# A two-layer diffusion backbone on one core: token tiles transposed in pairs, the second layer's gate made ahead of its attention, modulation columns by transposes

## The chip, the core and the metric

The kernel runs on one core of a Trainium2 chip. A core has five engines that run their own queues of instructions in order: TensorE (PE in the profile, with its weight loads shown apart as PEld), VectorE (DVE), ScalarE (ACT), GpSimd (POOL) and SyncE (SP), which here only issues DMA transfers. They work on SBUF, the on-chip memory of 128 partitions, and on PSUM, the banks that matmuls write. An engine that waits for another waits on a semaphore, and everything queued behind the waiting instruction on its engine waits with it.

The metric is the device time of one execution in microseconds, here 831.68 us as the median of three runs.

## The reference

The input is 512 latent tokens `x` and 256 context tokens `ctx`, 1024 wide, and two conditioning vectors, one for the latents and one for the context. There are two layers. Both modulate a normalised token, mix tokens by attention, gate the result, project it and add it back:

```python
h  = rms_norm(x,  pre_g[i]) * (1.0 + scale)  + shift     # shift, scale, gate = silu(c) @ ada_w[i] + ada_b[i]
hc = rms_norm(xc, pre_g[i]) * (1.0 + cscale) + cshift
...
x = x + gate * rms_norm(y, post_g[i])
if not last:
    xc = xc + cgate * rms_norm(yc, post_g[i])
```

The first layer's mixer is differential attention: 8 heads, each with two softmaxes of width 64, whose outputs are subtracted. The second is grouped-query attention with 8 query heads and 2 key/value heads of width 128, with a norm and a rotary position on queries and keys. In both a SiLU gate path `z` of the branch width multiplies the heads' output ahead of the output projection. In the second layer only the latents are wanted, the context gives keys and values alone. All inputs and the output are float32.

The modulation (`silu(c) @ ada_w[i] + ada_b[i]`) has three thirds: shift and scale, which the kernel needs as columns (features on partitions), and the gate, which it needs as a row that is the same on all partitions.

## The kernel before

**Arithmetic.** A float32 product is made of three float32r products: each operand is split into a high part (a cast to float32r) and a low part (the difference), and high by high, high by low and low by high are summed in PSUM. The helper `mm3` issues the three, and they are the rows L148, L149 and L150 of the profile. A weight comes in as float32 (`raw`, L209, a pool of two buffers named `raw` in SBUF), is cast on ACT (`whi`, L211), and its low part is made on POOL or DVE (`wlo`, L205). The stream of weights has a fixed order; a weight is loaded as soon as one of its slots is released.

**Order of the work.** Most of the code is generators that yield after each piece. In each layer a planner (`flow`) merges streams of steps: scores of a head (S), transposes of probabilities (T), products with V (M), odd steps (X), and one for the gate or modulation (A in the first layer, Y in the second). Each step has due times and lags against other steps; the time in between is filled with pieces of projections. The order of instructions on each engine is then set by the compiler's scheduler from that code and its priorities. It is fixed before the kernel runs.

**PSUM.** Four banks `bk` (68 to 71 in the listings below) are handed out in turn by `trp()` (for one use) and `pj()` (held until `close`). Two double banks `sc` (72 and 73) are handed out in turn by `sc2()`, and carry the attention scores.

**Modulation of both layers.** A section of the modulation is computed with `silu(c)` in one of four bands of 32 columns, so that its result stands in eight rows out of 128 (two vectors in each of four bands). `ada_red` (first layer, at the start; L498) and `ada1_finish` (second layer, inside the first layer's attention; L715) turn this into columns: a matmul of each 128x128 block against `sel32`, a 128x2 selector in float32, sums the bands. The profile counts each of those 16 and 16 float32 matmuls twice (x32 and x32). `gate0_finish` (L980) makes the first layer's gate as a row on all partitions by a float32 matmul against a 128x128 selector `selb`, two halves by two vectors, again counted twice (x8).

**Between the layers.** The output projection of layer one runs in three column windows (256, 256 and 512 wide). In the last, for each token tile m of 128 tokens (0 to 3 latents, 4 and 5 context), `resid_a` and `resid_b` norm the projection, add it to the token and norm that (`u`, L1169; `xn`, L1189, in two buffers). `h1_tr(m, j)` then transposes half of the tile, four blocks of 128x128, to one bank `bk` (L1196), modulates them with two instructions on DVE (L1202) and two on ACT (L1204), casts the result (L1206, ACT) and takes the low part (L1207, DVE): 12 calls. Those for tiles 0 to 3 stand in the loop over the last window, two tiles late; those for tiles 4 and 5 stand in the table `KV` as `('t', 4)` and `('t', 5)`, between the key (`'k'`) and value (`'v'`) projections of the six tiles and the transposes of keys (`'c'`).

**Second layer.** After the keys and values the weights' memory of that stage is released and a new SBUF pool, `t1q`, is opened in its place. The first pair of query heads is projected (`q_proj(0)`: matmuls to a `bk` bank, norm on ACT, rotary products `ta` and `tb` on DVE, L1241 and L1243, after which the bank is closed). Then `flow` runs the attention: `s1_units` makes scores to an `sc` tile, takes the row maximum on DVE (L1383), multiplies it (L1386), applies the exponential on ACT (`p`, L1389) and normalises. The gate of layer two is made on DVE: `gate1_part` loads 512 KB of `ada_w` (L1434) to one of the two `raw` buffers and multiplies its two 128x512 blocks by a column of `silu(c)` into an accumulator (L1442, L1444); four such parts make a half. `gate1_finish` sums a half over partitions by two matmuls, and adds and multiplies two rows (L1454, L1456). These ten steps are the stream Y, due behind the score steps 1, 3, 5, ... 19 of 32. The gate is first read by the output projection of layer two.

## Time and profile before

| what | value |
|---|---|
| median of three runs | 831.68 us (831.57 to 832.28) |
| profiled execution | 830.24 us |
| its span | 828.4 us (1.84 us of the execution lie outside) |
| PE busy | 794.2 us, 96% |
| DVE, ACT, POOL busy | 483.8, 456.6 and 435.5 us |
| granted PE clock over the span | 0.99 of full |
| layer one ends, last output window and first residuals begin | about 500 us |
| keys and values of layer two | 539 to 581 us |
| first queries | 581 to 605 us |
| attention of layer two | 605 to 780 us |

In the profile's rows `out<-in` names the tiles with their numbers left out, so that `h` is the high or low part of a token block, `hf` its float32 form, `gate` the accumulator of a gate, `sm` any small column. An arrow behind the idle time (`<-ACT p L1389`) names what ended the wait. Matmuls overlap, so the spacing of two starts says more of a matmul's price than its duration.

### The profile page before, as it was taken

The numbers are of one execution on the slowest core, as the hardware profiler recorded it, in microseconds if no ns is written. First come the engines' busy times: TensorE is split into PE (matmuls) and PEld (weight loads), VectorE is DVE, ScalarE is ACT, GpSimd is POOL, SyncE is SP. The second block draws the span as 40 slices with busy tenths as digits, with TensorE's granted clock in tenths as the row PEclk, the third lists the DMA queues.
The fourth block names the chain that finished last, engine by engine and source line by source line (L and its number), as shares of the span: only waits on it lengthen the run. The fifth ranks groups of instructions, "written<-read, shape, count | busy, mean of one in ns | idle before, by whom it ended". The sixth has DMA issues, their size and how long they took to land. (4 is left out here: it accounts for less than half of the span.)

```text
span 828.4 us, 14363 instructions
## 1 busy us (share of the span) xinstructions
PE 794.2 (96%) x5436; PEld 700.7 (85%) x5436; DVE 483.8 (58%) x909; ACT 456.6 (55%) x997; POOL 435.5 (53%) x612
## 2 busy tenths in 40 slices
PE   7999999999999999999999999889998989999997
PEld 4788897898878898878988898789998879899986
DVE  3745567664767426765278743764266676665634
ACT  5524457564665625855467643754464656666631
POOL 1124847965576752867633203575876746734201
PEclk9999999999999999999999999999999999999999
DMA  9924301212143331414210051121232340301112
GB/s 344 355 72 140 102 14 64 80 63 78 64 122 109 115 99 42 166 57 154 96 51 27 27 204 51 51 85 51 82 101 75 95 155 6 103 26 30 65 34 101
DMA packets 35236, 77.76 MB, mean 94 GB/s; under 512 B 3424, under 2 KB 10336, under 8 KB 35168
## 3 DMA queue, kind: packets, MB, share of 16 engines
q1 hardware_dynamic: 31600, 71.71, 26.0%
q10 hardware_dynamic: 3568, 5.16, 1.8%
q8 instruction: 42, 0.69, 0.4%
q14 instruction: 26, 0.21, 0.1%
HBM read 70.56 MB, written 2.10 MB: 88 GB/s over the span
## 5 line engine op out<-in xcount | busy, mean ns | idle before, releaser
L205 POOL TENSOR_TENSOR wlo<-raw,whi 128x256 fp32r<-128x256 f32 x196 | 148.4, 788 | 117.9 <-ACT whi L211 82.0
L148 PE MATMUL bk<-whi,h 128*128 128x256 f32 (+1 forms) x592 | 177.1, 301 | 5.6 <-DVE u L1169 2.0
L149 PE MATMUL bk<-wlo,h 128*128 128x256 f32 (+1 forms) x592 | 175.9, 298 | 0.3 <-DVE wlo L205 0.3
L150 PE MATMUL bk<-whi,h 128*128 128x256 f32 (+1 forms) x592 | 174.4, 298 | 0.8 <-DVE h L1207 0.8
L148 PE MATMUL bk<-h,whi 128*128 128x512 f32 (+2 forms) x416 | 147.1, 354 | 2.9 <-ACT sq L943 1.5
L149 PE MATMUL bk<-h,whi 128*128 128x512 f32 (+2 forms) x416 | 145.0, 349 | 0.0
L150 PE MATMUL bk<-h,wlo 128*128 128x512 f32 (+2 forms) x416 | 144.8, 349 | 0.0
L148 PEld LDWEIGHTS bk<-whi,h 128*128 128x128 f32 x592 | 112.3, 190 | 15.6 <-issue 3.6
L149 PEld LDWEIGHTS bk<-wlo,h 128*128 128x128 f32 x592 | 112.4, 190 | 4.0 <-DVE wlo L205 0.5
L150 PEld LDWEIGHTS bk<-whi,h 128*128 128x128 f32 x592 | 111.6, 189 | 4.8 <-DVE h L1207 1.2
L219 POOL TENSOR_SCALAR p<-p,sm 128x768 f32<-128x768 f32 (+1 forms) x80 | 67.2, 842 | 67.6 <-DVE sm L1390 23.4
L148 PEld LDWEIGHTS bk<-h,whi 128*128 128x128 f32 x416 | 78.4, 188 | 17.1 <-issue 5.4
L211 ACT CAST whi<-raw 128x1024 fp32r<-128x1024 f32 x64 | 67.3, 1051 | 46.2 <-PE bk L149 15.2
L150 PEld LDWEIGHTS bk<-h,wlo 128*128 128x128 f32 x416 | 78.3, 188 | 8.2 <-issue 1.3
L149 PEld LDWEIGHTS bk<-h,whi 128*128 128x128 f32 x416 | 78.5, 189 | 6.5 <-issue 0.3
L854 ACT ACTIVATE p<-sc,sm 128x768 f32<-128x768 f32 (+1 forms) x68 | 59.6, 880 | 29.7 <-DVE sm L851 29.6
L851 DVE TENSOR_REDUCE sm<-sc 128x1 f32<-128x768 f32 (+1 forms) x68 | 60.6, 918 | 17.0 <-PE sc L846 17.0
L205 POOL TENSOR_TENSOR sz<-sz,za 128x192 f32<-128x192 f32 (+1 forms) x48 | 32.1, 689 | 40.8 <-ACT za L185 40.8
L862 DVE SCALAR_TENSOR_TENSOR p<-p,sm,p 128x768 f32<-128x768 f32 (+1 forms) x34 | 39.0, 1146 | 24.3 <-POOL p L219 23.5
L914 ACT CAST ah<-bk 128x512 fp32r<-128x512 f32 x56 | 31.8, 590 | 31.6 <-PE bk L911 27.3
L915 DVE TENSOR_TENSOR al<-bk,ah 128x512 fp32r<-128x512 f32 x56 | 37.5, 684 | 17.5 <-ACT ah L914 17.3
L846 PE MATMUL sc<-qk,qk 64*128 64x384 f32 (+1 forms) x396 | 46.3, 360 | 1.4 <-ACT p L854 1.4
(236 smaller groups left out, 1683.6 us busy)
## 6 DMA issues: line engine op xcount, KB each, us to landing
raw<-in_a_w SPq DMA_DIRECT2D x28, 512.0 KB, 3.5
araw<-in_ada_w SPq DMA_DIRECT2D x12, 1024.0 KB, 5.3
raw<-in_b_w SPq DMA_DIRECT2D x20, 512.0 KB, 3.5
ag<-in_ada SPq DMA_DIRECT2D x16, 512.0 KB, 7.7
raw<-in_w_out SPq DMA_DIRECT2D x16, 512.0 KB, 3.5
sw<-qr ACTq DMA_DIRECT2D x32, 128.0 KB, 2.1
raw<-in_ada_w SPq DMA_DIRECT2D x8, 512.0 KB, 4.0
xnt<-in_xlT SPq DMA_DIRECT2D x4, 512.0 KB, 5.6
```

What stands on the lines that cost most here:

```text
L148: nc.tensor.matmul(o, ahi, bhi, start=start, stop=False)
L149: nc.tensor.matmul(o, ahi, blo, start=False, stop=False)
L150: nc.tensor.matmul(o, alo, bhi, start=False, stop=stop)
L205: eng.tensor_tensor(dst[:, i:i + n], a[:, i:i + n], b[:, i:i + n], op)
L211: nc.scalar.copy(hi, r)
L219: (nc.vector if eng == "v" else nc.gpsimd).tensor_scalar(dst, src, s_, 1.0, ALU.mult, ALU.mult)
L846: prev = nc.tensor.matmul(sc[m][:, j if nk == T else m, :w], a[r, tok], b[r, c], start=i == 0, stop=i == 2)
L851: nc.vector.tensor_reduce(mx, scv, AX.XY if nk == T else AX.X, ALU.max, negate=True)
L854: nc.scalar.activation(pv_, scv, AF.Exp, bias=mx, accum_out=l[:, m:m + 1])
L862: nc.vector.scalar_tensor_tensor(ps_[0], pt, r, ps_[0], ALU.mult, ALU.add)
L914: nc.scalar.copy(ah, tr)
L915: nc.vector.tensor_tensor(al, tr, f32(ah), ALU.subtract)
```

## The change

The diff has four parts.

1. `row_cols` takes the place of the `sel32` matmuls in `ada_red` and `ada1_finish`: it transposes each 128x128 block, and DVE sums the four bands from PSUM into a small tile.
2. `gate0_finish` splits its row into a high and a low float32r part (ACT and DVE, to tiles of the tag `tmp`, of which there are three, shared with other users) and issues two float32r matmuls where one float32 matmul stood. `selb` becomes float32r.
3. `h1_tr(p, j)` works on a pair of token tiles: eight transposes to a double bank `sc`, modulation 256 wide, and cast and low part for two blocks of features at a time. The calls for pairs 0 and 1 stand in the loop at its fourth and sixth tile, those for pair 2 in `KV` as `('t', 0)` and `('t', 1)`, where the second number is now the half. The order of keys and values in `KV` changes with it.
4. The eight calls of `gate1_part` are issued right behind `q_proj(0)`, ahead of the planner, with two buffers `gw` of their own in the pool `t1q`. `gate1_finish` stays in the stream Y, due behind score steps 6 and 12.

```diff
...
-KV = (('k', 0), ('k', 1), ('k', 2), ('k', 3), ('t', 4), ('v', 0), ('v', 1), ('k', 4), ('t', 5), ('c', 0), ('k', 5), ('c', 1), ('c', 2), ('c', 3), ('v', 3), ('v', 2), ('v', 5), ('c', 4), ('v', 4), ('c', 5))
+KV = (('k', 0), ('k', 1), ('k', 2), ('t', 0), ('k', 3), ('t', 1), ('v', 0), ('v', 1), ('c', 0), ('v', 2), ('c', 1), ('k', 4), ('c', 2), ('k', 5), ('c', 3), ('v', 3), ('v', 4), ('c', 4), ('v', 5), ('c', 5))
...
-GOFF = 1
-GSTEP = 2
+GFIN = (6, 12)
...
     nc.vector.tensor_copy(s32[:, :, 0:2], scv)
     sel32 = cp.tile([P, 2], F32, name="sel32", bufs=1)
     nc.vector.tensor_reduce(sel32, ident.rearrange("p (j r) -> p r j", j=4)[:, 0:2, :], AX.X, ALU.add)
-    selb = [cp.tile([P, P], F32, name=f"selb{v}", bufs=1) for v in range(2)]
+    selb = [cp.tile([P, P], F32R, name=f"selb{v}", bufs=1) for v in range(2)]
     for v in range(2):
         nc.vector.tensor_copy(selb[v], sel32[:, v:v + 1].to_broadcast([P, P]))
 
...
         row = st.tile([P, 512], F32, tag="row", name=nm("row"), bufs=1)[:, :n * P]
         nc.scalar.copy(row, o)
         close(o)
-        o = trp()
+        mods_set(k0, nb, row_cols(row, n).rearrange("p (w k v) -> p w v k", w=2, k=nb))
+
+    def row_cols(r, n):
+        o = trp()[:, :n * P]
         for b in range(n):
-            nc.tensor.matmul(o[:, b * 2:b * 2 + 2], row[:, b * P:(b + 1) * P], sel32, start=b == 0, stop=b == n - 1)
-        ov_ = o[:, :2 * n].rearrange("p (w k v) -> p w v k", w=2, k=nb)
-        mods_set(k0, nb, ov_)
+            nc.tensor.transpose(o[:, b * P:(b + 1) * P], r[:, b * P:(b + 1) * P], ident)
+        cols_ = small(2 * n)
+        nc.vector.tensor_reduce(
+            cols_.rearrange("p (b r) -> p b r", b=n), o.rearrange("p (b j r) -> p b r j", j=4, r=32)[:, :, 0:2, :], AX.X, ALU.add)
+        return cols_
 
     def mods_set(k0, nb, src):
         ks = slice(k0, k0 + nb)
...
 
         def ada1_finish(layer, sec):
             r = rows.pop((layer, sec))
-            o = trp()
-            for b in range(4):
-                nc.tensor.matmul(o[:, 2 * b:2 * b + 2], r[:, b * P:(b + 1) * P], sel32, start=b == 0, stop=b == 3)
-            ov_ = o[:, :8].rearrange("p (k v) -> p v k", v=2)
+            ov_ = row_cols(r, 4).rearrange("p (k v) -> p v k", v=2)
             mod_cols(layer, sec % 2, sec // 2, lambda v: ov_[:, v, :])
 
         qk, pend, qk_t = {}, {}, {}
...
             sl = slice(half * 512, half * 512 + 512)
             b = bcast(ada_b[0, 2 * D + half * 512:2 * D + half * 512 + 512])
             g = bcast(post_g[0, sl])
+            rh, rl = (t0.tile([P, 512], F32R, tag="tmp", name=nm("rg"), bufs=3) for _ in range(2))
+            nc.scalar.copy(rh, r)
+            nc.vector.tensor_tensor(rl, r, f32(rh), ALU.subtract)
             for v in range(2):
                 o = trp()
-                nc.tensor.matmul(o, selb[v], r, start=True, stop=True)
+                nc.tensor.matmul(o, selb[v], rh, start=True, stop=False)
+                nc.tensor.matmul(o, selb[v], rl, start=False, stop=True)
                 nc.vector.tensor_tensor(gate0[v][:, sl], o, b, ALU.add)
                 nc.vector.tensor_tensor(gate0[v][:, sl], gate0[v][:, sl], g, ALU.mult)
 
...
         nc.gpsimd.tensor_scalar(t, xd, r, 1.0, ALU.mult, ALU.mult)
         xn[m] = t
 
-    def h1_tr(m, j):
-        v = 0 if m < NQ else 1
-        tr = trp()
-        for k in range(4):
-            nc.tensor.transpose(tr[:, k * P:(k + 1) * P], xn[m][:, (j * 4 + k) * P:(j * 4 + k + 1) * P], ident)
-        hf = bp.tile([P, 4, P], F32, tag="hf", name=nm("hf"), bufs=1)
+    def h1_tr(p, j):
+        v = 0 if 2 * p < NQ else 1
+        tr = sc2().rearrange("p j (k n) -> p (j k) n", n=2 * P)
+        for i in range(2):
+            for k in range(4):
+                nc.tensor.transpose(tr[:, k, i * P:(i + 1) * P], xn[2 * p + i][:, (j * 4 + k) * P:(j * 4 + k + 1) * P], ident)
+        hf = bp.tile([P, 4, 2 * P], F32, tag="hf", name=nm("hf"), bufs=1)
         for k in range(4):
             kt = j * 4 + k
-            src, s_, h_ = tr[:, k * P:(k + 1) * P], mods[:, 1, v, 1, kt:kt + 1], mods[:, 1, v, 0, kt:kt + 1]
+            s_, h_ = mods[:, 1, v, 1, kt:kt + 1], mods[:, 1, v, 0, kt:kt + 1]
             if k < HFD:
-                nc.vector.tensor_scalar(hf[:, k, :], src, s_, h_, ALU.mult, ALU.add)
+                nc.vector.tensor_scalar(hf[:, k, :], tr[:, k, :], s_, h_, ALU.mult, ALU.add)
             else:
-                nc.scalar.activation(hf[:, k, :], src, AF.Identity, scale=s_, bias=h_)
-        hs = h1hi[:, j * 4:j * 4 + 4, m * P:(m + 1) * P]
-        nc.scalar.copy(hs, hf)
-        nc.vector.tensor_tensor(h1lo[:, j * 4:j * 4 + 4, m * P:(m + 1) * P], hf, f32(hs), ALU.subtract)
+                nc.scalar.activation(hf[:, k, :], tr[:, k, :], AF.Identity, scale=s_, bias=h_)
+        for a in (0, 2):
+            sl = slice(2 * p * P, 2 * p * P + 2 * P)
+            hs = h1hi[:, j * 4 + a:j * 4 + a + 2, sl]
+            nc.scalar.copy(hs, hf[:, a:a + 2])
+            nc.vector.tensor_tensor(h1lo[:, j * 4 + a:j * 4 + a + 2, sl], hf[:, a:a + 2], f32(hs), ALU.subtract)
 
     for i, m in enumerate(order):
         o = pj(n)
         run(out_proj(o, ghi, glo, w, m, n, 0, 4))
-        if i >= 2:
-            h1_tr(order[i - 2], 0)
+        if i in (3, 5):
+            h1_tr(i // 2 - 1, 0)
         run(out_proj(o, ghi, glo, w, m, n, 4, 8))
         resid_a(m, o)
-        if i >= 2:
-            h1_tr(order[i - 2], 1)
+        if i in (3, 5):
+            h1_tr(i // 2 - 1, 1)
         resid_b(m)
     ws.release(*wout_keys(0, c, n))
     pool_h.close()
...
         wv = None
         for what, m in KV:
             if what == "t":
-                hot(h1_tr, m, 0)
-                hot(h1_tr, m, 1)
+                hot(h1_tr, 2, m)
             elif what == "c":
                 k_tr(*ktr.pop(0))
             else:
...
 
         def gate1_part(half, k2):
             acc = gate1[:, half * 512:half * 512 + 512]
-            gw = wp.tile([P, 1024], F32, tag="raw", name=nm("raw"), bufs=2)
+            gw = t1q.tile([P, 1024], F32, tag="gw", name=nm("gw"), bufs=2)
             nc.sync.dma_start(
                 gw.rearrange("p (k n) -> p k n", k=2),
                 ada_w[1, k2 * 256:(k2 + 1) * 256, 2 * D + half * 512:2 * D + half * 512 + 512].rearrange("(k p) n -> p k n", p=P),
...
 
         add(q_proj(0))
         drain()
+        for i in range(8):
+            gate1_part(i // 4, i % 4)
         for kind, i in fill1:
             add({"q": q_proj, "z": z1_proj}[kind](i))
         S_, T_, M_, X_ = [], [], [], []
...
                 if h == KT - 1 and ch == 1:
                     T_.append(Step(tail1, 0.0, [(M_[-1], 0.0), (u[-1], 0.0)]))
                 pv1_steps(h, at, ch, u[-1], T_, M_)
-        Y_ = []
-        for i in range(10):
-            f = (lambda i=i: gate1_part(i // 5, i % 5)) if i % 5 < 4 else (lambda i=i: gate1_finish(i // 5))
-            Y_.append(Step(f, 0.9 if i % 5 == 4 else 0.0, [(S_[min(31, GOFF + GSTEP * i)], 0.0)], hot=False))
+        Y_ = [Step(lambda i=i: gate1_finish(i), 0.9, [(S_[GFIN[i]], 0.0)], hot=False) for i in range(2)]
         flow(1, [S_, T_, M_, X_, Y_])
         drain()
         w_o = w_o[0]
```

Three places show what this does to the queues. In the listings, tiles keep their numbers, and lines are each kernel's own (L148 and L1196 of before are L147 and L1202 of after).

PE, before, at the end of the last output window: `bk_71` is the projection of token tile 5, the transposes of `xn_5776` are those of tile 3.

```order
L150 MATMUL bk_71<-whi_5554,h_5072 128x512
L148 MATMUL bk_71<-whi_5554,h_5213 128x512
L149 MATMUL bk_71<-wlo_5555,h_5213 128x512
L150 MATMUL bk_71<-whi_5554,h_5214 128x512
L1196 MATMUL bk_70<-ident,xn_5776 128x128 x4
L148 MATMUL bk_71<-whi_5913,h_671_5297 128x256
L149 MATMUL bk_71<-wlo_5914,h_671_5297 128x256
L150 MATMUL bk_71<-whi_5913,h_672_5298 128x256
L148 MATMUL bk_71<-whi_5913,h_671_5297 128x256
```

PE, after, at the same place: `bk_69` is the projection of tile 5, `xn_5718` and `xn_5796` are tiles 2 and 3, and the matmuls to `bk_71` are the first key projection.

```order
L1202 MATMUL sc_73<-ident,xn_5796 128x128 x4
L149 MATMUL bk_69<-whi_5584,h_5102 128x512
L147 MATMUL bk_69<-whi_5584,h_5243 128x512
L148 MATMUL bk_69<-wlo_5585,h_5243 128x512
L149 MATMUL bk_69<-whi_5584,h_5244 128x512
L1202 MATMUL sc_72<-ident,xn_5718 128x128 x4
L1202 MATMUL sc_72<-ident,xn_5796 128x128 x4
L147 MATMUL bk_71<-whi_5923,h_684_5327 128x256
L147 MATMUL bk_70<-whi_5923,h_684_5327 128x256
```

The transposes of tiles 2 and 3 now go to the double banks `sc`, close together, and the last of them stand ahead of the first key projection as a group of eight.

SP, before, behind the weights of the first query pair: `raw_6820` and `raw_6999` are loads of the gate, the others weights of layer two.

```order
L209 DMA raw_6618<-in_b_w 128x1024
L209 DMA raw_6627<-in_b_w 128x1024
L209 DMA raw_6676<-in_b_w 128x1024
L1434 DMA raw_6820<-in_ada_w 128x2x512
L209 DMA raw_6904<-in_b_w 128x1024
L209 DMA raw_6913<-in_b_w 128x1024
L1434 DMA raw_6999<-in_ada_w 128x2x512
```

SP, after, from the same place on: `gw` are the loads of the gate.

```order
L1441 DMA gw_6636<-in_ada_w 128x2x512
L1441 DMA gw_6640<-in_ada_w 128x2x512
L208 DMA raw_6618<-in_b_w 128x1024
L1441 DMA gw_6644<-in_ada_w 128x2x512
L208 DMA raw_6627<-in_b_w 128x1024
L1441 DMA gw_6648<-in_ada_w 128x2x512
L1441 DMA gw_6652<-in_ada_w 128x2x512
L208 DMA raw_6708<-in_b_w 128x1024
L1441 DMA gw_6656<-in_ada_w 128x2x512
L1441 DMA gw_6660<-in_ada_w 128x2x512
```

The gate's first two loads now stand ahead of three weights behind which the first stood before, and seven of its eight loads come with three weights, where before two came with five.

DVE, before, from the third query tile of the first pair (`ta_6572`) on: the gate's first part (`gate_5296` from `raw_6820`) comes behind the fourth (`ta_6612`).

```order
L1241 TENSOR_TENSOR ta_6572<-bk_71,ropeb 128x256
L1243 TENSOR_TENSOR tb_6573<-bk_71,ropeb 128x2x64 x2
L1325 TENSOR_SCALAR qrs_6567<-qrs_6567 128x2
L1241 TENSOR_TENSOR ta_6612<-bk_69,ropeb 128x256
L1243 TENSOR_TENSOR tb_6613<-bk_69,ropeb 128x2x64 x2
L1325 TENSOR_SCALAR qrs_6607<-qrs_6607 128x2
L1442 TENSOR_SCALAR gate_5296<-raw_6820,scol 128x512
L1444 SCALAR_TENSOR_TENSOR gate_5296<-raw_6820,scol,gate_5296 128x512
L1344 TENSOR_TENSOR ql_6653<-bk_68,qh_6652 128x512
```

DVE, after, from the second query tile of the first pair: the multiplications of the gate, `gate_5326` from `gw`, stand between the rotary products of the query tiles.

```order
L1449 TENSOR_SCALAR gate_5326<-gw_6636,scol 128x512
L1451 SCALAR_TENSOR_TENSOR gate_5326<-gw_6636,scol,gate_5326 128x512
L1249 TENSOR_TENSOR ta_6532<-bk_71,ropeb 128x256
L1251 TENSOR_TENSOR tb_6533<-bk_71,ropeb 128x2x64 x2
L1451 SCALAR_TENSOR_TENSOR gate_5326<-gw_6640,scol,gate_5326 128x512 x2
L1249 TENSOR_TENSOR ta_6572<-bk_69,ropeb 128x256
L1251 TENSOR_TENSOR tb_6573<-bk_69,ropeb 128x2x64 x2
L1332 TENSOR_SCALAR qrs_6527<-qrs_6527 128x2
L1451 SCALAR_TENSOR_TENSOR gate_5326<-gw_6644,scol,gate_5326 128x512
L1332 TENSOR_SCALAR qrs_6567<-qrs_6567 128x2
L1451 SCALAR_TENSOR_TENSOR gate_5326<-gw_6644,scol,gate_5326 128x512
L1451 SCALAR_TENSOR_TENSOR gate_5326<-gw_6648,scol,gate_5326 128x512
```

Three parts of the gate and half of the fourth now stand ahead of the fourth query tile, where before none did; all eight stand ahead of the first maximum of scores, where before one did.

## The prediction

> **What bounds the kernel now.** I read the page's first lines, then a table of windows cut by stage, then what TensorE waited for, then the order of time at the costliest wait.
>
> ```profile
> span 828.4 us, 14363 instructions
> PE 794.2 (96%) x5436; PEld 700.7 (85%) x5436; DVE 483.8 (58%) x909; ACT 456.6 (55%) x997; POOL 435.5 (53%) x612
> ```
>
> TensorE is busy 96% of the span and idle for 34 us. Nothing else is near full. So two things shorten the kernel: less work on TensorE where it is never idle, or an end to its waits. The windows show which stage offers which (columns: window, length, then busy time of each engine, granted clock last but two).
>
> ```profile
> core 0: us, PE busy (x) PEld busy (x) DVE busy (x) ACT busy (x) POOL busy (x), PEclk, DMA share, GB/s
> 16.40:60.00 43.60, 42.59 (x289) 32.78 (x290) 24.62 (x52) 17.98 (x35) 12.60 (x16) 0.96 0.67 243
> 160.00:430.00 270.00, 267.47 (x1892) 230.49 (x1892) 155.24 (x280) 155.28 (x323) 168.44 (x219) 1.00 0.29 96
> 500.00:539.00 39.00, 36.18 (x171) 29.06 (x169) 21.99 (x35) 20.31 (x53) 18.61 (x36) 1.00 0.16 55
> 539.00:581.10 42.10, 39.34 (x317) 37.80 (x317) 22.37 (x57) 22.29 (x63) 26.63 (x39) 1.00 0.21 67
> 581.10:604.80 23.70, 23.70 (x179) 22.60 (x178) 7.19 (x22) 11.25 (x32) 20.73 (x34) 1.00 0.27 90
> 604.80:780.00 175.20, 166.46 (x1132) 155.59 (x1131) 115.94 (x233) 108.52 (x231) 96.62 (x131) 0.99 0.24 73
> ```
>
> Layer one's attention (160 to 430) has TensorE busy 99%: only its own work counts. The last output window and the keys and values (500 to 581) leave 2.8 and 2.8 us idle. The first queries (581 to 604.8) leave none, with DVE at 7.2 of 23.7 us. The second attention leaves 8.7 us. What TensorE waited for there:
>
> ```profile
> PE sc L148 <- ACT p L1389: 6.0, 3, 3.1
> PE bk L148 <- DVE u L1169: 2.0, 2, 1.3
> PE bk L148 <- ACT sz L1363: 1.6, 1, 1.6
> PE bk L148 <- ACT hf L1204: 1.1, 3, 0.6
> PE bk L1196 <- DVE u L1169: 0.9, 1, 0.9
> PE bk L150 <- DVE h L1207: 0.8, 2, 0.4
> PE bk L148 <- ACT h L1206: 0.6, 1, 0.6
> ```
>
> The rows give total, count and longest. Rows two, four, five, six and seven are the stage between the layers: 5.4 us. The other two are the second attention. The largest single wait, in order of time, with two windows behind it:
>
> ```profile
> 620.77 2.15 DVE L1444 SCALAR_TENSOR_TENSOR gate<-raw,scol,gate 128x512 f32<-128x512 f32 x2 [0.74 <-DMA raw<-in_ada_w]
> ...
> 624.58 0.77 DVE L1444 SCALAR_TENSOR_TENSOR gate<-raw,scol,gate 128x512 f32<-128x512 f32 x1
> 625.28 0.74 DVE L1386 TENSOR_TENSOR sm<-sm,qrs 128x1 f32<-128x1 f32 x1
> 625.94 0.76 DVE L1444 SCALAR_TENSOR_TENSOR gate<-raw,scol,gate 128x512 f32<-128x512 f32 x1
> 626.62 0.94 DVE L1383 TENSOR_REDUCE sm<-sc 128x1 f32<-128x768 f32 x1
> 627.19 0.58 PE L148 MATMUL sc<-kh,qh 128*128 128x384 f32 x1 [3.09 <-ACT p L1389]
> 627.20:629.00 1.80, 1.80 (x6) 1.80 (x7) 1.80 (x6) 0.00 (x0) 0.51 (x1) 0.54 0.64 223
> 629.00:631.00 2.00, 2.00 (x12) 2.00 (x11) 1.60 (x9) 0.79 (x1) 1.70 (x3) 0.56 0.15 61
> ```
>
> Here DVE waits 0.74 us for a load of the gate and multiplies for 3.7 us, and the column L1386 for the exponential stands behind it. TensorE waits 3.09 us for a score bank, and then its clock is granted at 0.54 and 0.56 for 3.8 us, which loses another 1.7.
>
> **Part one, modulation columns.**
>
> ```profile
> 308.88 0.40 PE L150 MATMUL bk<-h,wlo 128*128 128x512 f32 x1
> 309.11 0.95 PE L715 MATMUL bk<-sel,arow 128*128 128x2 f32 x8
> 309.92 0.64 PE L911 MATMUL bk<-ident,p 128*128 128x128 f32 x4
> 310.31 0.48 PE L148 MATMUL bk<-h,whi 128*128 128x512 f32 x1
> ```
>
> From start to start, four columns (eight issues) take 0.81 us and four transposes 0.39. Each `ada1_finish` therefore saves 0.42 on TensorE: four of them 1.7 us, all in busy time. The Trainium skill, page "TensorE: Matmul & The Clock Gate", section "Part 4: PE-mode transpose", gives about 275 ns for a 128x128 transpose in a kernel; taken as a price each, an estimate from that figure is 4.4 us for sixteen against 3.2 now, a loss of 1.2 us and a forecast of 822.3 in place of 819.4. The trace lets a run of four last 0.64 us but starts the next work after 0.39, so I go by the trace. The sums that DVE adds (eight, over 32 or fewer numbers per partition) read little; the nearest rows are L1386's 0.74 and L1383's 0.94, so at most 1 us each, and DVE has 115 us free in that window. In layer one nothing waits soon for layer two's columns, so they cost nothing; without that cover they would add at most 4.
>
> At the start, five `ada_red` make 16 columns: 1.7 us of TensorE at the same saving. Their results are waited for, and DVE's sum lengthens that chain, so the bounds are −1.7 and +1; I take −0.6, since TensorE is busy 42.59 of 43.60 us in that window.
>
> **Part two, the first gate.**
>
> ```profile
> 207.71 1.13 PE L980 MATMUL bk<-arow,selb 128*128 128x512 f32 x2
> 208.67 0.60 PE L911 MATMUL bk<-ident,p 128*128 128x128 f32 x4
> ```
>
> A float32 matmul of 512 columns takes 0.96 us from start to start. A float32r one takes 0.23 (308.88 to 309.11, above), and two replace it: 0.96 − 0.46 = 0.5 us, four times, −2.0. The cast and the difference that are added run on ACT and DVE, both under 60% busy in that window; the low part may come late for the second half's matmuls by up to 1 us. Parts one and two together in layer one: −3.7, bounds −4 and −2.
>
> **Part three, pairs between the layers.** TensorE issues the same 48 transposes.
>
> ```profile
> L1202 DVE TENSOR_SCALAR hf<-bk,mods 128x128 f32<-128x128 f32 x24 | 8.7, 406 | 1.8 <-PE bk L1196 1.2
> L1204 ACT ACTIVATE hf<-bk,mods 128x128 f32<-128x128 f32 x24 | 9.7, 453 | 10.4 <-DVE hf L1202 10.2
> L1207 DVE TENSOR_TENSOR h<-hf,h 128x512 fp32r<-128x512 f32 x12 | 10.1, 840 | 8.7 <-ACT h L1206 8.7
> L219 DVE TENSOR_SCALAR gT<-bk,subg 128x256 f32<-128x256 f32 x24 | 11.4, 476 | 1.4 <-ACT sq L932 1.2
> ```
>
> Twelve of each 256-wide modulation replace 24. By L219, also a scalar operation from PSUM, DVE would need 12 × 0.48 = 5.7 in place of 24 × 0.41 = 9.7: −4. ACT gains alike. Casts and low parts keep count and size. More important, `u` (L1169) no longer shares banks with the transposes, which go to the idle `sc`. So the waits on `u`, `hf` and `h` (5.4 us) should end. What is late next: a pair's transposes wait for both tiles' `xn`, and with two `xn` buffers the third tile's norm waits for the first pair's transposes. Pair 2's modulations also stand in DVE's order ahead of keys' products, which hold banks for the value projections; I count three such waits of 0.3 to 1.4 us. Following the new order with the old durations, the last value projection ends 4.5 to 5.6 us earlier. I take −4.5, with bounds −6 and +2 (all stalls kept, and those three waits added).
>
> **Part four, the second gate.**
>
> ```profile
> L1444 DVE SCALAR_TENSOR_TENSOR gate<-raw,scol,gate 128x512 f32<-128x512 f32 x14 | 12.3, 879 | 5.0 <-DMA raw<-in_ada_w 4.8
> raw<-in_ada_w SPq DMA_DIRECT2D x8, 512.0 KB, 4.0
> 665.45 0.34 SPq L209 DMA_DIRECT2D raw<-in_b_w  x1
> 667.02 7.44 SPq L1434 DMA_DIRECT2D raw<-in_ada_w  x2
> ```
>
> Leaving the attention are the three waits for the exponential (6.0), the half clock (1.7), and probably the 1.6 us for `sz`: its weights (issued at 665.45) stood on SP behind gate loads that waited for a `raw` buffer. That is 9.3 us at most. Score steps have further limits there, so I take two thirds: −6.
>
> The cost comes earlier. The first `gw` loads overlie the value projections' weight memory, so they start only when those end; weights behind them on SP wait too. A load takes 4.0 us, a part about 1.5 on DVE (two of 0.76 or 0.77), and two buffers carry eight loads: four rounds of about 5.5 us, or 22 us, about the length of the first queries (23.7). DVE's 12 us of work fit beside 7.2. But queued behind each wait for a load are the rotary products `ta` and `tb`, which release the banks of the query projections. Walking the order gives TensorE two waits, of at most 0.6 and of 1.6 to 2.8 us, and later first scores. I take +2.5, with bounds 0 and +14. Part four: −3.5.
>
> **Sum.** −3.7 − 0.6 − 4.5 − 3.5 = −12.3. Against the profiled execution's 830.24 us: 817.9. That execution lies 1.4 us under the median of 831.68, so on the median's basis 819.4.
>
> **Rivals.**
>
> *One of the two scheduling gains fails.* The pairs bring new waits where the old ones went, or the second attention's waits return with other releasers, since its DVE still works 116 of 175 us. For it speaks that only 2.8 us are idle in each window of part three; against, that the new banks really are free there. Without part three 823.9, without part four 822.9.
>
> *More comes back.* The queries hide all gate work, and all 9.3 us return: 819.4 − 2.5 − 3.3 = 813.6.
>
> *Slower: the gate's loads hold the queries.* In each round DVE waits for a load with the rotary products behind it, and TensorE idles as at 624 to 627, 3.1 us plus 1.7 of half clock. Four rounds cost 19.2 in place of 2.5: 836.1. Sign turns at 14.8, three such rounds. For it: two buffers for eight loads, 4.0 us each, and no idle time in that stage now to absorb it. Against: DVE is idle for 16 of 23.7 us and four PSUM banks let queries run ahead. The Trainium skill, page "TensorE: Matmul & The Clock Gate", section "Part 1: The HAM clock gate", has the clock fall after an idle window of about 3.4 us; this trace shows the fall after 3.1.
>
> **How the numbers follow.** The forecast as worked out, 815.5 to 823: 0.45. One scheduling gain missing, 823 to 828: 0.22. More comes back, 810 to 815.5: 0.13. The slower mechanism, whole or in part, 828 and up: 0.20, of which 0.17 is above 833. The range from 811 to 831 leaves out 0.02 below and 0.18 above. Faster and slower mean by over 0.2% (1.7 us), about what a measurement can tell: faster 0.8, same 0.03, slower 0.17.
>
> **What would show it.** Right: transposes of four in 0.4 us at `ada1_finish`; no wait on `u` between 500 and 540; values finished 8 to 9 us earlier than now (about 4 from layer one, 4.5 from this stage); no gate product behind the first scores; no wait over 3 us and no half clock in the second attention. Wrong: TensorE waiting in the first queries for `tb` or for a score bank, with DVE waiting for `gw` at the same time, over 3 us at once; or new waits for `xn` or `kn` as long as those on `u`.

## The result

The changed kernel takes 834.3 us in the median of 20 runs, the kernel before 831.71 in 20 runs beside it: a ratio of 1.0036, 95% interval 1.0024 to 1.0049. It is slower by 0.36%, where −1.5% was forecast. The profiled execution of the changed kernel took 831.91 us, span 830.1, the lowest of its runs; the differences below are of that one profile against the one before.

The windows of the changed kernel, cut at the same points of the program as those shown of before:

```profile
16.40:60.00 43.60, 39.62 (x265) 29.42 (x261) 23.85 (x55) 18.06 (x35) 13.02 (x16) 1.00 0.65 243
161.20:430.90 269.70, 268.11 (x1883) 230.13 (x1883) 159.41 (x284) 155.89 (x325) 167.32 (x219) 1.00 0.29 96
430.90:506.90 76.00, 68.28 (x501) 63.53 (x501) 48.04 (x82) 43.41 (x98) 19.30 (x29) 0.96 0.19 70
506.90:544.90 38.00, 38.00 (x192) 31.53 (x191) 19.51 (x29) 19.27 (x49) 17.70 (x37) 1.00 0.17 53
544.90:584.10 39.20, 36.50 (x298) 35.22 (x297) 20.76 (x50) 18.29 (x55) 26.15 (x37) 1.00 0.23 74
584.10:608.60 24.50, 23.97 (x178) 22.42 (x177) 15.88 (x29) 11.82 (x33) 22.83 (x30) 1.00 0.65 214
608.60:781.90 173.30, 166.35 (x1133) 156.05 (x1132) 111.20 (x226) 109.15 (x233) 99.09 (x135) 0.99 0.17 56
```

Between the layers TensorE no longer waits at all in the last output window (38.00 of 38.00 us; 36.18 of 39 before). But the stage ahead of it, the end of layer one, takes 76 us where 70 stood before, at a mean clock of 0.96. To see where time goes although the two kernels run the same work in other orders, I added up TensorE's matmuls, each at the median spacing of its shape, leaving out those that parts one and two replace, and compared the times at which both kernels had done the same amount:

| stage | forecast | changed − before | with own column buffers (below) − before |
|---|---|---|---|
| start, to 60 us | −0.6 | +1.0 | +1.1 |
| layer one, to 425 us | −3.7 | −0.2 | −2.9 |
| end of layer one, to 500 us | 0 | +6.1 | −1.2 |
| between the layers, keys and values, to 580 us | −4.5 | −3.9 | −4.2 |
| first queries and first scores, to 620 us | +2.5 | +7.0 | +7.2 |
| second attention, to 782 us | −6.0 | −8.2 | −7.3 |
| sum | −12.3 | +1.8 | −7.3 |

Two rows carry the miss. The larger is the end of layer one, which no part of the change touches. TensorE's longest waits there, and its wait in the first queries:

```profile
PE sc L847 <- ACT p L855: 5.5, 2, 4.1
PE bk L147 <- DVE tb L1251: 3.5, 2, 2.9
```

In order of time, DVE and TensorE of the changed kernel at the end of layer one, and the windows behind the wait (granted clock last but two):

```profile
451.00 0.95 DVE L947 TENSOR_TENSOR gT<-gT,sq 128x768 f32<-128x768 f32 x1
451.86 5.20 DVE L995 TENSOR_TENSOR h<-gT,h 128x768 fp32r<-128x768 f32 x4
456.99 0.94 DVE L852 TENSOR_REDUCE sm<-sc 128x1 f32<-128x768 f32 x1
...
456.81 0.33 PE L912 MATMUL bk<-ident,p 128*128 128x128 f32 x1 [0.51 <-ACT sz L817]
461.21 1.01 PE L847 MATMUL sc<-qk,qk 64*128 64x256 f32 x6 [4.07 <-ACT p L855]
...
457.00:461.00 4.00, 0.14 (x1) 0.00 (x0) 4.00 (x6) 4.00 (x8) 0.00 (x0) 0.73 0.00 0
461.00:463.00 2.00, 1.53 (x8) 1.02 (x8) 2.00 (x5) 2.00 (x7) 0.00 (x0) 0.50 0.00 0
463.00:466.00 3.00, 3.00 (x16) 3.00 (x17) 2.86 (x6) 2.04 (x6) 2.71 (x3) 0.56 0.52 175
```

DVE makes four low parts of gated heads (L995, 5.2 us) ahead of the row maximum of the last head (L852). The exponential waits for the maximum, the next scores wait for the exponential, and TensorE idles 4.07 us; then its clock is at half for about 5 us. Before the change two low parts stood there, ahead of a maximum of the context (128x256), and the latents' last maxima were already done. DVE's queue before:

```
L990 TENSOR_TENSOR h_5048<-gT_810,h_5047 128x768
L990 TENSOR_TENSOR h_5052<-gT_1279,h_5051 128x768
L851 TENSOR_REDUCE sm_4975<-sc_72 128x1
```

and after the change:

```
L995 TENSOR_TENSOR h_5078<-gT_820,h_5077 128x768
L995 TENSOR_TENSOR h_5082<-gT_1289,h_5081 128x768
L995 TENSOR_TENSOR h_5086<-gT_1685,h_5085 128x768
L995 TENSOR_TENSOR h_5090<-gT_2415,h_5089 128x768
L852 TENSOR_REDUCE sm_4967<-sc_72 128x1
```

TensorE's order differs too. It writes the latents' last scores 7.7 us later, behind a group of projections; before:

```profile
444.49 1.32 PE L846 MATMUL sc<-qk,qk 64*128 64x384 f32 x12
```

and after the change:

```profile
452.18 1.32 PE L847 MATMUL sc<-qk,qk 64*128 64x384 f32 x12
```

Both together, the late scores and the low parts ahead of their maximum, are called the late order below.

### The profile page after: what moved, and what is told of

It reads as the page before. It is cut to its first block, busy times and chain, and to the rows that moved or that the text cites. A ratio compares the mean times of both kernels' runs of the same rounds, so it can differ in the third digit from the quotient of the medians.

```text
span 830.1 us, 14282 instructions
## 1 busy us (share of the span) xinstructions
PE 791.6 (95%) x5404; PEld 696.2 (84%) x5404; DVE 488.7 (59%) x908; ACT 453.5 (55%) x987; POOL 441.5 (53%) x612
## 5 line engine op out<-in xcount | busy, mean ns | idle before, releaser
L204 POOL TENSOR_TENSOR wlo<-raw,whi 128x256 fp32r<-128x256 f32 x196 | 150.4, 798 | 103.7 <-ACT whi L210 68.0
L147 PE MATMUL bk<-whi,h 128*128 128x256 f32 (+1 forms) x592 | 177.3, 302 | 8.3 <-DVE tb L1251 3.5
L148 PE MATMUL bk<-wlo,h 128*128 128x256 f32 (+1 forms) x592 | 175.8, 299 | 0.0
L147 PE MATMUL bk<-h,whi 128*128 128x512 f32 (+2 forms) x416 | 147.3, 354 | 3.0 <-DVE gT L218 1.2
L148 PE MATMUL bk<-h,whi 128*128 128x512 f32 (+2 forms) x416 | 144.7, 348 | 0.0
L147 PEld LDWEIGHTS bk<-whi,h 128*128 128x128 f32 x592 | 112.6, 190 | 18.3 <-issue 4.5
L148 PEld LDWEIGHTS bk<-wlo,h 128*128 128x128 f32 x592 | 112.7, 191 | 3.4
L218 POOL TENSOR_SCALAR p<-p,sm 128x768 f32<-128x768 f32 (+1 forms) x80 | 67.4, 845 | 74.8 <-DVE sm L858 34.7
L147 PEld LDWEIGHTS bk<-h,whi 128*128 128x128 f32 x416 | 78.2, 188 | 15.7 <-issue 2.4
L148 PEld LDWEIGHTS bk<-h,whi 128*128 128x128 f32 x416 | 78.3, 188 | 8.7 <-issue 2.4
L852 DVE TENSOR_REDUCE sm<-sc 128x1 f32<-128x768 f32 (+1 forms) x68 | 60.7, 916 | 22.9 <-PE sc L847 22.9
L1415 DVE TENSOR_TENSOR al<-bk,ah 128x512 fp32r<-128x512 f32 x48 | 32.1, 685 | 25.7 <-ACT ah L1414 24.8
L916 DVE TENSOR_TENSOR al<-bk,ah 128x512 fp32r<-128x512 f32 x56 | 37.5, 683 | 16.4 <-ACT ah L915 16.3
```

What stands on the lines that cost most here:

```text
L147: nc.tensor.matmul(o, ahi, bhi, start=start, stop=False)
L148: nc.tensor.matmul(o, ahi, blo, start=False, stop=False)
L204: eng.tensor_tensor(dst[:, i:i + n], a[:, i:i + n], b[:, i:i + n], op)
L218: (nc.vector if eng == "v" else nc.gpsimd).tensor_scalar(dst, src, s_, 1.0, ALU.mult, ALU.mult)
L852: nc.vector.tensor_reduce(mx, scv, AX.XY if nk == T else AX.X, ALU.max, negate=True)
L916: nc.vector.tensor_tensor(al, tr, f32(ah), ALU.subtract)
```

## Each part alone

The first question was which part brings that late order, and what each part is worth. Each of four kernels holds the lines of one part of the diff and nothing else of it. The kernel before was timed again beside each group of kernels. Its median was 831.49 to 831.71 us in four groups and 832.92 in one, that of the runs whose text gives 832.92, so medians of that group and of another compare only to about 1.4 us.

**Part one.**

```diff
-            nc.tensor.matmul(o[:, 2 * b:2 * b + 2], r[:, b * P:(b + 1) * P], sel32, ...)
+            nc.tensor.transpose(o[:, b * P:(b + 1) * P], r[:, b * P:(b + 1) * P], ident)
+        cols_ = small(2 * n)
+        nc.vector.tensor_reduce(cols_..., o..., AX.X, ALU.add)
```

> Only part one of the change (modulation columns by transposes and a DVE sum). Theory A, from comparing the two traces: this part alone brings the late order at the end of layer one, where the row maximum of the last head stands behind four low parts of the gated heads on DVE: a TensorE wait of about 4 us near 457, then half clock, together +6 us there, +1 us at the start, and -1.5 us of TensorE work: 836 to 838 us against about 831.7. Theory B (the late order comes from the gate's tiles or from all parts together): no wait over 2 us there, and 829.5 to 831 us.

839.57 us against 831.57, ratio 1.0095 (1.0075 to 1.0115). The wait of 4.07 us is there and ends at 462.06; between 425 and 500 us the kernel loses 7.1 us, and it is 8.8 behind at 500. Nothing of it comes back later: theory A, somewhat above its number.

**Part two.**

```diff
-                nc.tensor.matmul(o, selb[v], r, start=True, stop=True)
+                nc.tensor.matmul(o, selb[v], rh, start=True, stop=False)
+                nc.tensor.matmul(o, selb[v], rl, start=False, stop=True)
```

> Only part two (layer one's gate by two float32r matmuls each). Theory A: the work saved on TensorE shows, and nothing else moves: -1 to -2 us, 829.7 to 830.7 us. Theory B: savings within layer one's attention are taken back by the next wait of a fixed order, since scores wait for other engines there: within 0.5 us of before.

831.05 against 831.57, ratio 0.9997 (0.9983 to 1.001). By 425 us it is 1.1 us ahead, by 437 us 0.3 behind: theory B by its number. But in the profile it is not a wait that takes the saving back. TensorE waits as long as before, 1.57 us against 1.56; here its clock is at half for 3.4 us from then on, and the saving is gone by 430 us. Part two alone:

```profile
426.70 1.12 PE L911 MATMUL bk<-ident,p 128*128 128x128 f32 x4 [1.57 <-DVE al L915]
426.40:429.80 3.40, 3.10 (x15) 3.10 (x16) 3.20 (x11) 1.59 (x5) 0.91 (x1) 0.50 0.00 0
```

The kernel before:

```profile
427.79 0.66 PE L911 MATMUL bk<-ident,p 128*128 128x128 f32 x4 [1.56 <-DVE al L915]
427.80:431.20 3.40, 3.40 (x29) 3.01 (x30) 3.09 (x11) 1.27 (x3) 0.92 (x1) 1.00 0.02 5
```

That is one profiled execution of each; whether the other runs lose the saving in the same way is not shown.

**Part three.**

```diff
-    def h1_tr(m, j):
+    def h1_tr(p, j):
-        tr = trp()
+        tr = sc2().rearrange("p j (k n) -> p (j k) n", n=2 * P)
```

> Only part three (token tiles transposed in pairs, with the new order of keys and values). Theory A: the 4 us that the changed kernel wins between 518 and 590 us belong to this part and reach the end: about 827.5 us. Theory B: they were only the late tail of layer one being caught up (its loads were ready earlier relative to TensorE), and alone the part gives under 1 us.

838.05 against 831.57, ratio 1.0072 (1.0048 to 1.0097). Neither theory: alone, the pairs made the kernel slower. Its profile (833.59 us, the lowest of its runs) shows the forecast gain, 4.5 us between 522 and 546 us, and then a loss of 8 us in the second attention, by new waits (the other runs took 836.7 to 840.2, so that the profile shows less of the loss than the median):

```profile
PE bk L1406 <- DVE tb L1246: 2.1, 1, 2.1
PE bk L1406 <- DVE al L1410: 1.6, 2, 0.9
PE bk L1406 <- DVE ql L1346: 1.3, 1, 1.3
PE bk L148 <- ACT sz L1365: 1.2, 1, 1.2
```

Three of the four are waits for DVE, in a stage that the part doesn't touch. The clock adds to them: it is at half from 623.6 to 630.5 us and from 671.4 to 674.8 (granted 0.51 and 0.50), where the kernel before has half clock for 3.4 us alone, from 627.3. The 6.9 us more at half speed are an estimated 3.4 of the 8 us.

**Part four.**

```diff
-            gw = wp.tile([P, 1024], F32, tag="raw", name=nm("raw"), bufs=2)
+            gw = t1q.tile([P, 1024], F32, tag="gw", name=nm("gw"), bufs=2)
...
+        for i in range(8):
+            gate1_part(i // 4, i % 4)
...
```

> Only part four (layer two's gate ahead of its attention). Theory A: it costs 7 us in the first queries (a wait of some 3 us for the rotary products, and half clock) and returns 8 us in the attention: about -1 us, 830 to 831.5 us. Theory B: the wait at the first queries hangs on the new order of keys and values; alone it is under 1 us and the part gains 5 us or more, 826 us.

825.92 against 831.57, ratio 0.9937 (0.9918 to 0.9957): theory B. In the first queries it is 3.2 us behind (7.0 in the changed kernel), with waits of 1.62 and 0.81 us in place of one of 2.95, and the clock stays whole (1.00 from 600 to 612 us).

The four parts alone add up to +8.0 − 0.5 + 6.5 − 5.7 = +8.3 us, the changed kernel measured +2.6. They don't add.

## Is it the place of the column sums?

A reading of the queues showed that the late order comes and goes with one thing in part one: whether the small result of DVE's sum takes its place in the ring of 24 small tiles (`small`, which row maxima and their scales use) or in a tile of its own.

```diff
-        cols_ = small(2 * n)
+        cols_ = sm.tile([P, 8], F32, tag="cols", name=nm("cols"), bufs=2)[:, :2 * n]
```

> The changed kernel with one thing different: the small result of the DVE sum has two buffers of its own and does not take turns in the ring of 24 small tiles, which the row maxima and their scales use too. In the order of DVE two, not four, low parts of the gated heads then stand ahead of the last head's row maximum, as before the change. Theory A (that order is the cause of the 4 us wait and the half clock behind it): the stall near 457 goes, 6 to 7 us are won, 827 to 828.5 us. Theory B (the transposes and the sum themselves, or the cheaper gate, bring the stall): over 832 us.

821.71 us against 832.92, ratio 0.9871 (0.9852 to 0.9891). One line, 32 bytes per partition and buffer, turns the changed kernel from 0.36% slower to 1.3% faster. The long waits of this kernel:

```profile
PE bk L147 <- DVE tb L1251: 3.3, 1, 3.3
PE bk L1411 <- DVE al L1415: 1.9, 1, 1.9
PE bk L147 <- DVE kn L1282: 1.7, 2, 0.9
...
PE sc L847 <- ACT p L855: 1.4, 1, 1.4
```

The 4.1 us are gone, and the last column of the table shows that layer one, the stage between the layers and the second attention then come out near the forecast; the first queries, at +7.2, do not. The gain is more than the stall: 2.7 us more of layer one's savings arrive too. (By the profiles the kernel is 7.8 us under before, by the medians 11.2: the profiled run of before, 830.24, is below its medians, and the median of before in this group is the highest of all groups.) The gain is above theory A's 6 to 7 us.

To tell the ring from the transposes, the kernel before got nothing but a copy, with its selector matmuls left as they were:

```diff
+            cols_ = small(8)
+            nc.vector.tensor_copy(cols_, o[:, :8])
-            ov_ = o[:, :8].rearrange("p (k v) -> p v k", v=2)
+            ov_ = cols_.rearrange("p (k v) -> p v k", v=2)
```

> The kernel before with one small copy added: layer two's columns, still made by the selector matmuls, are copied by DVE from PSUM to a tile of the ring of 24 small tiles ahead of their use (four copies of 128x8). In DVE's order four low parts then stand ahead of the last head's row maximum. Theory A (a tile of that ring in this place brings the late order, whatever makes it): +5 to +7 us, 836.5 to 838.5, with a wait of about 4 us near 455. Theory B (it takes the transposes or the freed TensorE time): under +1 us.

838.17 against 831.58, ratio 1.0078 (1.0065 to 1.0092): theory A. DVE stands as in the changed kernel:

```profile
452.83 5.20 DVE L992 TENSOR_TENSOR h<-gT,h 128x768 fp32r<-128x768 f32 x4
457.95 0.94 DVE L853 TENSOR_REDUCE sm<-sc 128x1 f32<-128x768 f32 x1
...
PE sc L848 <- ACT p L856: 5.5, 2, 4.1
```

The same copy to a tile of its own:

```diff
+            cols_ = sm.tile([P, 8], F32, tag="cols", name=nm("cols"), bufs=2)
+            nc.vector.tensor_copy(cols_, o[:, :8])
```

> As the run before it, with the four copies going to a tile of their own with two buffers. The order at the end of layer one is then the one before the change. Theory A: within 1 us of before, 831 to 832.5 us. Theory B (an added DVE instruction in that place is enough): as the run with the ring.

828.74 against 831.58, ratio 0.9963 (0.9949 to 0.9977). Faster than before by 2.8 us, where at most 1 us either way was expected, though work was added. Where the 2.8 us come from is not shown: the order at the end of layer one is that of before, and the profiled execution, 829.79, is only 0.45 us under that of before. And part one alone with its own tile, the same edit as in the changed kernel:

```diff
-        cols_ = small(2 * n)
+        cols_ = sm.tile([P, 8], F32, tag="cols", name=nm("cols"), bufs=2)[:, :2 * n]
```

> Part one alone, with the column sums in a tile of their own with two buffers. Three low parts stand ahead of the last head's row maximum, between the two (before) and the four (part one alone with the ring, 839.6 us). Theory A: most of the 7.5 us go, 831 to 834 us. Theory B (the transposes are the price): over 837 us.

827.58 against 831.58, ratio 0.9952 (0.9939 to 0.9964). The part that cost 8.0 us with the ring gains 4.0 without it, more than theory A had. Three low parts stand ahead of a maximum in this run too, but it is one of the context, and TensorE's longest wait at the end of layer one is 1.5 us: the number of low parts alone is not the price. So three pairs of kernels that differ in the ring alone differ by 12.6, 9.4 and 12.0 us in their medians (changed kernel, copy, part one). Counted by stages as above, the end of layer one, 425 to 500 us, makes 7.3, 6.9 and 6.7 us of it; the rest lies mostly ahead of it.

Part one left out of the changed kernel:

```diff
+            nc.tensor.matmul(o[:, 2 * b:2 * b + 2], r[:, b * P:(b + 1) * P], sel32, ...)
-            ov_ = row_cols(r, 4).rearrange("p (k v) -> p v k", v=2)
```

> The changed kernel without part one: modulation columns by the selector matmuls as before. Theory A (part one alone costs 7.5 us and nothing else hangs on it): 826 to 828 us. Theory B (the late order at the end of layer one comes with the cheaper gate as well): over 832 us.

826.36 against 832.92, ratio 0.9934 (0.9914 to 0.9955): theory A.

One run tried to show the price of DVE's queue directly, by moving two of the four low parts to GpSimd in the changed kernel:

```diff
-                nc.vector.tensor_tensor(b, gT[kt], f32(a), ALU.subtract)
+                pieces(nc.gpsimd if kt in (2, 3) else nc.vector, b, gT[kt], f32(a), ALU.subtract)
```

> The changed kernel with one thing different: at the end of layer one the low parts of the gated heads 2 and 3 are made on GpSimd (two of the four that stood ahead of the last head's row maximum on DVE). Up to that place the order of all engines is the changed kernel's. Theory A (DVE's queue ahead of the row maximum is the price): the wait near 457 and the half clock go, 5 to 7 us are won, 827.5 to 829.5 us, and not the 821.7 of the kernel whose column sums have their own buffers, since about 3 us of that came earlier in layer one. Theory B (the stall hangs on something else that the small ring holds up): over 833 us.

833.5 against 831.49, ratio 1.0028 (1.0012 to 1.0045): theory A's number failed, and the time is in theory B's range, hardly under the changed kernel's 834.3. Its waits at the end of layer one:

```profile
PE bk L912 <- DVE gT L218: 2.5, 1, 2.5
PE sc L847 <- ACT p L855: 1.7, 1, 1.7
...
455.91 6.30 POOL L204 TENSOR_TENSOR h<-gT,h 128x256 fp32r<-128x256 f32 x6
```

The wait for the exponential shrank from 4.1 to 1.7 us, as DVE's queue explains it. But GpSimd took 6.3 us for the two low parts, a DVE instruction behind them waited, and the copy that frees a bank (L218) came late: 2.5 us of new wait. The run neither confirms that the low parts ahead of the maximum are the whole price nor refutes it.

## Pairs and the second gate together, and what the gate costs

> Parts three and four alone, without parts one and two. Theory A (the stages stand apart: -4 us between the layers, +7 and -8 around the first queries): about 826.5 us. Theory B (the parts alone measured +6.5 and -5.6 us, and they add): 832.4 us. Theory C: with the gate out of the attention nothing is left there that the pairs can upset, and both gains are whole: 821 to 823 us.

Its diff is parts three and four, shown above. 826.87 against 832.92, ratio 0.9936 (0.9919 to 0.9953): theory A. Beside part four alone (ratio 0.9937) the pairs add nothing to it: 4.5 us are won in the last output window and at the first keys, and 8.2 us lost in the first queries in place of 3.2.

Then the changed kernel with its own column buffers, but the second gate as before:

```diff
-            gw = t1q.tile([P, 1024], F32, tag="gw", name=nm("gw"), bufs=2)
+            gw = wp.tile([P, 1024], F32, tag="raw", name=nm("raw"), bufs=2)
...
-        for i in range(8):
-            gate1_part(i // 4, i % 4)
...
```

> Parts one, two and three with the column sums in buffers of their own, the second gate as before the change. Theory A (pairs lose their gain in the second attention as long as the gate's parts are there): 5 us or so are lost against 821.7, 826 to 831 us, with new waits on DVE between 610 and 700 us. Theory B (the loss that pairs showed alone was that one order's bad luck): 817 to 822 us.

826.43 against 831.49, ratio 0.9932 (0.9918 to 0.9947): theory A. Part four is worth 4.7 us on top of the rest by the two medians, 6.2 by the differences against the kernel before of each group.

What in part four is worth it? The kernel before with own buffers for the gate, its parts left in the attention in the code:

```diff
-            gw = wp.tile([P, 1024], F32, tag="raw", name=nm("raw"), bufs=2)
+            gw = t1q.tile([P, 1024], F32, tag="gw", name=nm("gw"), bufs=2)
```

> The kernel before with one thing different: the gate's loads have two buffers of their own, as in part four, but its parts stay in the attention where they were. Theory A (part four gains because the multiplications leave the attention): only the waits for the loads go, -1 to -2 us, 829.5 to 831 us. Theory B (it gains because loads of the gate and weights no longer share two buffers): about 826 us, all that part four gives alone.

828.15 against 832.92, ratio 0.995 (0.9932 to 0.9967): 4.8 us of the 5.7 (3.4 against the 831.57 beside which the 5.7 were measured), closer to theory B, but not for its reason. The gate's multiplications in this kernel, and in the kernel before:

```profile
L1444 DVE SCALAR_TENSOR_TENSOR gate<-gw,scol,gate x14: 739/1034/1129, 586.5 to 607.9; 128x512 f32<-128x512 f32 x14
```

```profile
L1444 DVE SCALAR_TENSOR_TENSOR gate<-raw,scol,gate x14: 740/752/1368, 603.4 to 680.1; 128x512 f32<-128x512 f32 x14
```

The rows give minimum, median and maximum in ns, and the first and last start. With own buffers alone the scheduler moves all parts to 586 to 608 us, ahead of the attention. The buffers set the place, not the place in the code. The same holds on top of the other parts. This is the changed kernel with its own column buffers; the gate keeps its two load buffers, and its parts go back to the attention in the code:

```diff
-        cols_ = small(2 * n)
+        cols_ = sm.tile([P, 8], F32, tag="cols", name=nm("cols"), bufs=2)[:, :2 * n]
...
-        for i in range(8):
-            gate1_part(i // 4, i % 4)
...
```

> As the changed kernel with its own column buffers, but the gate's parts stay in the attention, with two load buffers of their own. A try at both gains: the loads no longer hold weights up, and fewer parts stand in the first queries. Theory A (the first queries' 7 us come from where the parts stand): 818 to 820 us. Theory B (early loads and parts are as costly there as in the changed kernel, since the scheduler still moves them up): 821 to 824 us.

822.34 against 831.49, ratio 0.9888 (0.9868 to 0.9907): theory B, as with the parts placed ahead (0.9871).

Last, the 7 us that the first queries cost. In the changed kernel, DVE in those queries:

```profile
600.34 1.23 DVE L1451 SCALAR_TENSOR_TENSOR gate<-gw,scol,gate 128x512 f32<-128x512 f32 x1 [1.31 <-DMA gw<-in_ada_w]
...
607.24 1.05 DVE L1451 SCALAR_TENSOR_TENSOR gate<-gw,scol,gate 128x512 f32<-128x512 f32 x1 [2.16 <-DMA gw<-in_ada_w]
...
612.12 0.47 DVE L1251 TENSOR_TENSOR tb<-bk,ropeb 128x128 f32<-128x128 f32 x2
...
612.64 0.58 PE L147 MATMUL bk<-whi,h 128*128 128x256 f32 x1 [2.95 <-DVE tb L1251]
612.50:615.00 2.50, 2.36 (x11) 2.36 (x12) 2.50 (x6) 0.46 (x2) 2.40 (x3) 0.50 0.89 351
```

The waits for loads stand there, and the rotary product behind them. To price them, six of the gate's eight loads were left out of the changed kernel with its own column buffers; all sixteen multiplications stay and use the data of the first two loads again:

```diff
...
+            if len(gws) < 2:
+                gws.append(t1q.tile([P, 1024], F32, tag="gw", name=nm("gw"), bufs=2))
+                nc.sync.dma_start(...)
+            gw = gws[k2 % 2]
```

> As the changed kernel with its own column buffers, but six of the gate's eight loads are left out: the eight parts multiply the first two loads' data again and again, so the second layer's gate is made of the wrong numbers. The multiplications stay. Theory A (the 7 us in the first queries are DVE's waits for gate loads, with the rotary products behind them): 5 to 7 us less, 815 to 817 us, and no wait for the rotary products over 0.5 us. Theory B (the multiplications themselves fill DVE there): 820 to 822 us.

818.15 against 831.49, ratio 0.9834 (0.9814 to 0.9854): between the theories. It is 3.6 us under the kernel with own columns by the two medians, 2.1 by the differences against the kernel before of each group. The wait for the rotary products is still 2.25 us, where theory A had under 0.5, but here the clock stays whole behind it:

```profile
590.53 2.44 DVE L1455 SCALAR_TENSOR_TENSOR gate<-gw,scol,gate 128x512 f32<-128x512 f32 x2
592.89 0.41 DVE L1249 TENSOR_TENSOR ta<-bk,ropeb 128x256 f32<-128x256 f32 x1
...
593.95 0.36 PE L147 MATMUL bk<-whi,h 128*128 128x256 f32 x1 [2.25 <-DVE tb L1251]
593.60:596.00 2.40, 2.05 (x17) 2.08 (x18) 2.40 (x4) 0.00 (x0) 2.40 (x3) 1.00 0.54 188
```

DVE waits for no load from 582 to 600 us here, so what the rotary product stands behind is multiplications alone. Counted by stages, the first queries cost 4.2 us in this run and 7.2 with all eight loads: about 3 of the 7 us are the loads' waits with the half clock behind them. What makes the rest, DVE's multiplying or the order, was not separated. Smaller loads, in the changed kernel with its own column buffers, sixteen of 256 KB in place of eight of 512:

```diff
...
-            gw = t1q.tile([P, 1024], F32, tag="gw", name=nm("gw"), bufs=2)
+            gs = t1q.tile([P, 512], F32, tag="gw", name=nm("gw"), bufs=4)
...
+        for i in range(16):
+            gate1_part(i // 8, i % 8)
```

> The changed kernel with its own column buffers (821.7 us) and the gate's loads cut in half: sixteen of 256 KB to four buffers of half the size, the same memory. Theory A (the price in the first queries is DVE's wait for a whole load of 512 KB in a queue of two): 1 to 3 us less, 818.5 to 820.5 us. Theory B (the sum of the loads' time sets it): 821 to 823 us.

819.95 against 831.58, ratio 0.9853 (0.9839 to 0.9867): theory A's size, and the fastest complete kernel of the study. But its interval overlaps with that of the whole loads (0.9852 to 0.9891), and against the kernel before of each group it gains 11.6 us where they gain 11.2, so a gain over the whole loads is not shown. Its long waits in that stage are others:

```profile
PE sc L147 <- ACT p L1396: 2.8, 1, 2.8
PE sc L147 <- ACT qh L1350: 2.1, 1, 2.1
```

## Why the prediction was wrong, step by step

- *What bounds the kernel*: right. TensorE's work and its waits are what every run moved.
- *Parts one and two, −3.7 in layer one*: this step failed. The prices were right: four transposes take 0.35 us from start to start (309.60 to 309.95) where four columns took 0.81, and DVE's sums took 0.17 to 0.19 us each, where at most 1 was counted. The sentence that failed is "In layer one nothing waits soon for layer two's columns, so they cost nothing". Nothing waits for their values. But they took places in a ring that the row maxima of the scores use, and with that the scheduler wrote the end of layer one in the late order: +6.1 us where the prediction had no term at all. The copy added to the kernel before shows that the ring suffices for it; the transposes aren't needed. With its own tile the step measured −2.9 and −1.2 for the two stages, against −3.7 and 0 forecast.
- *The start, −0.6*: +1.0 in the profile. It can't be put down to part one: the run without that part (all but the columns) is also 1.0 us behind there, the pairs alone 0.1, and the granted clock from 16.4 to 60 us is 1.00 in the changed kernel, 0.93 in the run without part one and 0.96 before. One profile of each can't tell a microsecond at the start.
- *Part three, −4.5*: right within the changed kernel, −3.9, and −4.2 with own columns. The three waits behind the keys' products that it counted came too (two on `kn`, 1.8 us in all, and one of 0.7 on `vl`). Wrong was to think that it stays won: alone, it was lost again in the second attention, in part by the clock.
- *Part four, −6 and +2.5*: the gain was −8.2, the cost +7.0. The mechanism and the place of the cost were those forecast, a wait of DVE for a gate load with the rotary products behind it (2.95 us against 1.6 to 2.8), but the half clock behind that wait, and the multiplications at a mean of 1.08 us each where 0.76 were counted, were not in the sum. So the part came to −1.2 where −3.5 was forecast. The rival that the loads hold the queries had that clock in it, but counted four such rounds, and one came.
- *The rivals*: none named layer one's end. The slower rival had the right sign and the wrong place; that the time came out within 2 us of its 836.1 is luck.
- *The signs named ahead*: those of the two scheduling gains came: no wait on `u` between the layers, and from 618 us on no half clock and no wait over 1.7 us. The values were to end 8 to 9 us earlier; they ended 3.0 later, because of the loss at the end of layer one.

Why a tile of that ring makes the scheduler write the late order stays open. The number of buffers in the ring is not the reason: with 20, 22, 26, 28 or 32 of them the order at the end of layer one stays what it is in either kernel, and with 1, 3, 4 or 8 buffers of its own the column sum leaves the order as with two. That the late order itself costs the 6 us is shown by its trace and by three pairs of kernels that have it and don't, not by a run that changes that order alone.

## What to carry to other kernels

Where a scheduler writes the order, an edit's price is not only its instructions: compare the whole queues of before and after, above all in stages that the edit doesn't touch, and look at which engine's queue puts work for later ahead of something that is waited for now. In this kernel a new small result cost 9 to 13 us more with a place in a ring that the critical chain uses than with its own buffers, so try both. Four small added copies moved the median by 2.8 us, so don't read a difference of that size as the price of an edit without its trace, and look in it for stretches of half clock first. Parts that are measured one by one don't add. Buffers, more than the place in the code, decided here when the gate, for which nobody waits, was made.

## What the runs showed that was not expected

- The clock's fall doesn't go by the length of one wait. Waits of 4.07, 3.09 and 2.95 us were followed by half clock, the wait of 2.25 us in the run with six loads left out was not; but a wait of 2.12 us in the run with halved loads was:

```profile
600.57 0.44 PE L147 MATMUL sc<-kh,qh 128*128 128x384 f32 x1 [2.12 <-ACT qh L1350]
602.50:605.00 2.50, 2.50 (x10) 2.50 (x9) 2.36 (x7) 0.63 (x1) 2.33 (x4) 0.50 0.22 56
```

Two waits of like length had unlike outcomes at one place of the program, 1.57 us with half clock and 1.56 without (part two alone and the kernel before, above). The stretches of half clock named here last 3.4 us (from 426.4 with part two alone, from 627.3 before) or 6.9 (from 623.6 with the pairs alone).

The Trainium skill, page "TensorE: Matmul & The Clock Gate", section "Part 1: The HAM clock gate", gives about 3.4 us of idle time and a window that runs freely. The free window fits two like waits with unlike outcome; the length does not fit, as 2.12 and 1.57 us sufficed.
- A float32 transpose of 128x128 costs TensorE 0.11 us in a run of four (0.60 us of duration for all), and a 128x2 float32 matmul of two issues 0.2 us.
- The same multiplication on DVE took a median of 752 ns spread over the attention and 1034 ns when done ahead of it (in the kernel before, with shared and with own load buffers); in the changed kernel GpSimd is busy for 22.8 of 24.5 us there. Seven traces were compared instruction by instruction (before, changed, part four alone, own load buffers, own columns, six loads left out, smaller loads). Eleven multiplications ran with GpSimd at work for under 0.4 of their time, and all eleven took 737 to 753 ns; each one over 800 ns had GpSimd at work for two thirds of its time or more. The gate's loads are not the reason: with six of the eight left out the median was 1184 ns. A run without GpSimd's work there was not made, so GpSimd as the cause is likely and not shown.
